# Full 128-row matmuls for the second rotary score product and for the row broadcasts of a six-layer forward pass

## The chip, the cores and the metric

The kernel runs on one core of one Trainium2 chip. The metric is the device time of one execution in microseconds; the time before is 2570.8 us, the median of three runs (2565.99 to 2572.75).

## The reference, cut to what matters

One sequence of 512 tokens, 1024 features, goes through six layers: pooling, gated delta rule, latent attention, pooling, then a layer with a state-space mixer beside a convolution, and a differential attention. All arithmetic is float32. Three of them matter here.

Latent attention (16 heads): each query and key has a part of 128 without position and a rotary part of 64; the rotary key is shared by all heads.

```python
q = jnp.concatenate([q_nope, q_rope], axis=-1)
k = jnp.concatenate([k_nope, jnp.broadcast_to(k_rope, (B, S, MLA_HEADS, MLA_ROPE))], axis=-1)
...
s = jnp.einsum('bqhd,bkhd->bhqk', q_blk, k).astype(jnp.float32) * scale
s = jnp.where(kpos[None, :] <= qpos[:, None], s, -jnp.inf)
p = jax.nn.softmax(s, axis=-1)
```

Gated delta rule (8 heads) and state-space mixer (16 heads): per head a cumulative sum over tokens of a log decay, and from it a matrix of decays between pairs of tokens.

```python
g = jnp.cumsum(g.reshape(B, N, C, H).transpose(0, 3, 1, 2), axis=-1)
diff = g[..., :, None] - g[..., None, :]
decay = jnp.exp(jnp.where(causal, diff, -jnp.inf))
```

## The kernel before, in words

Activations lie with features on the 128 partitions and the 512 tokens in the free dimension. All weights stream from HBM in slabs of 512 KB through `load_w` (L268): SyncE issues the load, ScalarE rounds the slab to a high part (L278), VectorE or GpSimd subtracts to get the low part (L279). A projection (`proj`, `projn`) calls `mm3` (L282 to L287) for every 128x128 tile of weights: high times high, high times low, low times high, each one float32r matmul. These three lines are most of TensorE's work. Plain float32 matmuls (the scores L1096, the transposes L1007, the weighted values L1011) run in two passes and show as two instructions.

The layers are written as two streams: projection units for a later head, and generators for an earlier head's attention or recurrence, which `weave` or `step` advance by a few yields after each unit. The order of instructions on each engine is then set by a planner when the program is built, from dependences and its own model of time; it also places all waits. So attention matmuls stand between the projection's matmuls on TensorE, and TensorE takes its instructions in the order that the planner wrote.

Rotary scores (`attend` in `mla`, L1084): `stacked` (L976) makes for each head of a pair one tile of 128 rows. For head i the 64 rows of its own half (`rs`) hold the high part of the rotary query, the other 64 rows its low part. `krh` and `krl` are the high and the low part of the rotary key, which stands twice in 128 rows. For each block of 128 queries three products accumulate in one bank: L1096 (128 rows, float32), L1097 (all 128 rows against `krh`: high and low query in one), and L1098 (the 64 rows `rs` against `krl`: high query times low key). With 16 heads and four query blocks each of the lines stands for 64 products, of 128, 256, 384 and 512 key columns. VectorE's mask (L1099) and the softmax wait for the third.

Row broadcasts: `cumsums` (L575) makes the cumulative sums once per layer in both layouts, and with `hi, lo` (L591 to L593) a high and a low part of the sums with one head per row and tokens in columns, 8 or 16 rows, both tiles in the buffers of the tag "rope" (three of them). `row_bcast` (L596) spreads the row of one head over 128 partitions: a stationary operand that picks the row (a column of the identity `self.sel`, repeated 128 times) times `hi` (L599), and the same times `lo` (L600) on top, into one bank of 512 columns. It is called in `k_chain` (gated delta, 8 heads, bank a), in `rec` (the same 8 heads, bank b), and in `ssd` (16 heads, bank b); `decay_t` on VectorE, or ScalarE's L1295 and L1299, read the bank.

Between `k_chain` and the recurrence lies `inverse` (L831): a chain of VectorE steps with small loads and stores through DRAM, beside which the convolutions of the projections (L552) run on VectorE too.

Of the kernel before, what the change touches and what calls it, by code (L numbers as in the profile page):

```python
# [10 lines left out]
F32 = mybir.dt.float32  # L11
F32R = mybir.dt.float32r
I32 = mybir.dt.int32
AF = mybir.ActivationFunctionType
ALU = mybir.AluOpType
# [4 lines left out]
P = 128  # L20
S = 512
# [34 lines left out]
def _consts():  # L56
    i = np.arange(P)
    ident = np.eye(P, dtype=np.float32)
    triu = (i[:, None] <= i[None, :]).astype(np.float32)
    maskt = np.where(i[:, None] <= i[None, :], 0.0, NEG).astype(np.float32)  # L60
    maskq = np.where(i[None, :] <= i[:, None], 0.0, NEG).astype(np.float32)
    lev = []
    for b in (32, 64):
        jb, ib = i[:, None] // b, i[None, :] // b
        lev.append(((jb % 2 == 0) & (ib == jb + 1)).astype(np.float32))
    b64 = ((i[:, None] // 64) == (i[None, :] // 64)).astype(np.float32)
    rc = np.zeros((P, 4, 16), np.float32)
    for n, w in enumerate(WINDOWS):
        rc[:, n, :] = 1.0 / np.minimum(np.arange(16) + 1, w)
    inv1 = (np.float32(10000.0) ** (-np.arange(32, dtype=np.float32) / np.float32(32))).astype(np.float32)  # L70
    r = i % 32
    f = (i % 64) // 32 * 16 + r % 16
    mcol = np.stack([inv1[f], np.where(r < 16, -1.0, 1.0)], 1).astype(np.float32)
    inv2 = (np.float32(500000.0) ** (np.float32(-2.0) * np.arange(8, dtype=np.float32) / np.float32(16))).astype(np.float32)
    d = i % 64
    dcol = np.stack(
        [np.where(d < 16, inv2[d % 8], 0.0), np.where(d < 8, -1.0, 1.0)], 1
    ).astype(np.float32)
    parts = [
        ("ident", ident), ("triu", triu), ("maskt", maskt), ("maskq", maskq),  # L80
        ("lev1", lev[0]), ("lev2", lev[1]), ("b64", b64),
        ("rc", rc.reshape(P, -1)),
        ("mrope", mcol), ("drope", dcol),
    ]
    return parts
# [107 lines left out]
class Net:  # L193
    def __init__(self, ctx, tc, a, poff, coff, first=()):
        self.tc, self.nc, self.a = tc, tc.nc, a
        nc = self.nc
        self.cp = ctx.enter_context(tc.tile_pool(name="cp", bufs=1))
        self.wp = ctx.enter_context(tc.tile_pool(name="wp", bufs=3))
        self.bp = ctx.enter_context(tc.tile_pool(name="bp", bufs=1))
        self.sp = ctx.enter_context(tc.tile_pool(name="sp", bufs=2))  # L200
        self.dp = ctx.enter_context(tc.tile_pool(name="dp", bufs=1, space=DRAM))
        self.pm = ctx.enter_context(tc.tile_pool(name="pm", bufs=4, space=PSUM))
        self.n = 0
        npar = a["params"].shape[1]
        ncon = a["consts"].shape[1]
        n0 = poff["norm"][1]
        par = self.cp.tile([P, npar], F32, name="par")
        con = self.cp.tile([P, ncon], F32, name="con")
        self.par, self.poff, self.con, self.coff = par, poff, con, coff
        self.x = [self.cp.tile([P, S], F32, name=f"x{i}") for i in range(8)]  # L210
        self.loaded, self.rest = [], nc.vector
        nc.sync.dma_start(par[:, :n0], a["params"][:, :n0])
        nc.sync.dma_start(self.x[0], a["xt"][0])
        ahead = [self.load_w(slab, D) for slab in first]
        self.loaded = ahead[:1]
        for i in range(1, 8):
            nc.sync.dma_start(self.x[i], a["xt"][i])
        nc.scalar.dma_start(par[:, n0:], a["params"][:, n0:])
        nc.scalar.dma_start(con, a["consts"])
        self.ones = self.cp.tile([P, P], F32, name="ones")  # L220
        nc.vector.memset(self.ones, 1.0)
        self.sel = self.cp.tile([16, 16], F32R, name="sel")
        nc.vector.tensor_copy(self.sel, self.c("ident")[:16, :16])
        self.bias = {}

    def p(self, name, i=0, n=1):
# [347 lines left out]

    def cumsums(self, gn, nh):  # L575

        nc = self.nc
        ps = self.ps("b")
        v = ps[:, : 4 * nh].rearrange("p (c h) -> p c h", c=4)
        nc.tensor.matmul(v, self.c("triu"), gn, start=True, stop=True)  # L580
        cs = self.small([P, 4, nh], "cs", 1)
        nc.vector.tensor_copy(cs, v)
        ps2 = self.ps("b")
        v2 = ps2[:, : 4 * nh].rearrange("p (c h) -> p c h", c=4)
        nc.tensor.matmul(v2, self.ones, gn, start=True, stop=True)
        last = self.small([P, 4, nh], "last", 1)
        nc.vector.tensor_copy(last, v2)
        pr = self.ps("b")
        for c in range(NC):
            nc.tensor.matmul(pr[:nh, c * P : (c + 1) * P], gn[:, c, :], self.c("triu"), start=True, stop=True)  # L590
        hi, lo = self.big("rope", F32R, [16, S]), self.big("rope", F32R, [16, S])  # L591
        nc.scalar.copy(hi[:nh], pr[:nh])
        nc.vector.tensor_tensor(lo[:nh], pr[:nh], hi[:nh].bitcast(F32), op=ALU.subtract)  # L593
        return cs, last, (hi, lo)

    def row_bcast(self, h, nh, rows, bank):  # L596
        ps = self.ps(bank)
        sel = self.sel[:nh, h : h + 1].to_broadcast([nh, P])
        self.nc.tensor.matmul(ps, sel, rows[0][:nh], start=True, stop=False)  # L599
        self.nc.tensor.matmul(ps, sel, rows[1][:nh], start=False, stop=True)  # L600
        return ps

    def decay_t(self, gb, cs, h, tag):
# [12 lines left out]
    def gdn(self, gnext):  # L616
        nc, a = self.nc, self.a
# [23 lines left out]
        cs, last, rows = self.cumsums(abn[:, :, 32:40], 8)  # L641
# [20 lines left out]
        def k_chain(heads):  # L662
            pn = self.ps("c")
            vn = pn[:, :16].rearrange("p (h c n) -> p h c n", h=4, n=1)
            for i, hd in enumerate(heads):
                kT[hd] = sil.pop(hd)
                (_, sq) = self.sq_add(None, kT[hd])
                self.tok_sums(sq, self.ones[:, 0:1], vn[:, i])
                yield 1
            ssq = self.small([P, 4, 4], "ssq", 1)  # L670
            nc.vector.tensor_scalar(ssq, vn[:, :, :, 0], EPS, None, op0=ALU.add)
            h0 = heads[0]
            nc.vector.reciprocal(bk[:, h0 : h0 + 4], ssq)
            nc.vector.tensor_tensor(
                bk[:, h0 : h0 + 4], bk[:, h0 : h0 + 4], beta.rearrange("p c h -> p h c")[:, h0 : h0 + 4], op=ALU.mult
            )
            nc.vector.tensor_copy(sk[:, h0 : h0 + 4], ssq)
            rk = self.tok_rsqrt(ssq, "rk")
            nc.vector.tensor_tensor(sk[:, h0 : h0 + 4], sk[:, h0 : h0 + 4], rk, op=ALU.mult)
            for hd in heads:  # L680
                k = kT[hd]
                gb = self.row_bcast(hd, 8, rows, "a")
                dt = self.decay_t(gb, cs, hd, "c")
                yield 1
                kk = self.ps("a")
                for c in range(NC):
                    sl = slice(c * P, c * P + P)
                    nc.tensor.matmul(kk[:, sl], k[:, sl], k[:, sl], start=True, stop=True)
                m = self.big("y")
                for c in range(NC):  # L690
                    sl = slice(c * P, c * P + P)
                    nc.vector.scalar_tensor_tensor(
                        m[:, sl], kk[:, sl], bk[:, hd, c : c + 1], dt[:, sl], op0=ALU.mult, op1=ALU.mult
                    )
                mt[hd] = m
                yield 1
# [39 lines left out]
        def rec(hd):  # L736
            st = heads.pop(hd)
            q, vN = st["q"], st["v"]
            yield 1
            gb = self.row_bcast(hd, 8, rows, "b")  # L740
            qe = self.big("c")
            nc.scalar.activation(qe, gb, AF.Exp)
            nc.vector.tensor_tensor(qe, q, qe, op=ALU.mult)
# [3 lines left out]
            for c in range(NC):  # L747
                sl = slice(c * P, c * P + P)
# [11 lines left out]
            for c in range(NC):  # L760
                sl = slice(c * P, c * P + P)
# [254 lines left out]
    def mla(self, gnext):  # L1016
        nc, a = self.nc, self.a
# [66 lines left out]
        def attend(hp, st, vN):  # L1084
            q, k = st["q"], st["k"]
            for i in range(2):
                hd = hp * 2 + i
                rs = slice(i * 64, i * 64 + 64)
                po = self.ps("c")
                vh = [v[:, (hd % 4) * P : (hd % 4) * P + P] for v in vN]  # L1090
                prev = None
                for qb in range(NC):
# [2 lines left out]
                    ps = self.ps("a")  # L1095
                    nc.tensor.matmul(ps[:, :n], q[i][:, sl], k[i][:, :n], start=True, stop=False)  # L1096
                    nc.tensor.matmul(ps[:, :n], q[2][i][:, sl], krh[:, :n], start=False, stop=False)  # L1097
                    nc.tensor.matmul(ps[:, :n], q[2][i][rs, sl], krl[rs, :n], start=False, stop=True)  # L1098
                    nc.vector.tensor_tensor(ps[:, sl], ps[:, sl], self.c("maskq"), op=ALU.add)  # L1099
                    pr, rcp = self.softmax_rows(ps, n, qs[:, qb])  # L1100
                    nc.vector.tensor_scalar(pr[:, :n], pr[:, :n], rcp, None, op0=ALU.mult)
# [40 lines left out]
    def even(self, gnext):  # L1142
# [101 lines left out]
        def ssd(g, st):  # L1244
# [42 lines left out]
            for i in range(2):  # L1287
                po = self.ps("a")
                for hh in range(2):
                    hd = 4 * g + 2 * i + hh  # L1290
                    gb = self.row_bcast(hd, 16, rows, "b")
                    w = self.big("c")
                    for c in range(NC):
                        sl = slice(c * P, c * P + P)
# [255 lines left out]
```

## Time and profile before

| | us |
|---|---|
| median of three runs | 2570.8 |
| the profiled execution | 2575.46 |
| its span, first to last instruction | 2573.7 |
| TensorE matmul busy | 2476.2 (96%) |
| TensorE weight load busy | 1976.5 (77%) |
| VectorE busy | 1628.0 (63%) |
| ScalarE busy | 1062.2 (41%) |
| GpSimd busy | 466.2 (18%) |

The mean granted clock of TensorE is 0.983 of full speed; the DMA engines move 80 GB/s on average. Busy is the union of an engine's instruction times over the span; TensorE's matmul times overlap each other, since each record holds until the modelled end of its results. By stages of the span: first pooling layer to about 320 us, gated delta to 915, latent attention to 1480 (its scores from 1100 to 1395), second pooling to 1785, state-space layer to 2245, differential attention to the end.

### The profile page before, as it was taken

How to read it: one execution, taken by the hardware profiler on the slowest of the kernel's cores; microseconds unless marked ns; L12 is line 12 of the kernel's file. 1: busy time of each engine (PE TensorE's matmuls, PEld its weight loads, DVE VectorE, ACT ScalarE, POOL GpSimd, SP SyncE). 2: the span in 40 equal slices, each digit the busy share in tenths (PEclk: the TensorE clock that was granted, in tenths of full speed). 3: DMA queues.
4: the chain of work that ended last, by engine and by line, in shares of the span. 5: the costliest groups of instructions: out<-in, count | busy, mean ns of one | idle time of the engine just before them, and what ended most of it. 6: DMA issues, size and time to landing. Idle time of an engine off the chain costs nothing. (4 is left out here: it accounts for less than half of the span.)

```text
span 2573.7 us, 30632 instructions
## 1 busy us (share of the span) xinstructions
PE 2476.2 (96%) x11692; PEld 1976.5 (77%) x11692; DVE 1628.0 (63%) x2874; ACT 1062.2 (41%) x1676; POOL 466.2 (18%) x374
## 2 busy tenths in 40 slices
PE   8999999688899999999999999999999999999999
PEld 6888877476777888887787888887777767877877
DVE  6675368678556454355557366744997888477774
ACT  4333354134335343444445332333235546365553
POOL 0121103222321110000000112203334443200000
PEclk9999999799999999999999999999999999999999
DMA  4323224311211232211111233232222211321122
GB/s 152 98 91 99 94 82 127 100 36 46 80 56 58 90 95 97 86 60 56 62 58 53 95 98 95 94 100 88 83 88 67 67 50 58 113 66 58 58 64 76
DMA packets 81907, 205.63 MB, mean 80 GB/s; under 512 B 28352, under 2 KB 28480, under 8 KB 81760
## 3 DMA queue, kind: packets, MB, share of 16 engines
q1 hardware_dynamic: 81264, 202.23, 24.7%
q8 instruction: 92, 1.51, 0.2%
q0 software_dynamic: 208, 0.66, 0.1%
q10 hardware_dynamic: 288, 0.79, 0.1%
q14 instruction: 55, 0.45, 0.1%
HBM read 196.30 MB, written 7.34 MB: 79 GB/s over the span
## 5 line engine op out<-in xcount | busy, mean ns | idle before, releaser
L285 PE MATMUL psmm<-h,wh 128*128 128x512 f32 x1704 | 691.1, 406 | 47.9 <-DVE t L552 32.0
L278 ACT CAST wh<-wr 128x1024 fp32r<-128x1024 f32 (+3 forms) x366 | 376.6, 1030 | 779.2 <-PE psmm L286 591.5
L286 PE MATMUL psmm<-h,wh 128*128 128x512 f32 x1704 | 686.5, 403 | 0.1
L287 PE MATMUL psmm<-h,wl 128*128 128x512 f32 x1704 | 684.1, 401 | 0.0
L279 DVE TENSOR_TENSOR wl<-wr,wh 128x1024 fp32r<-128x1024 f32 (+2 forms) x270 | 322.1, 1193 | 185.9 <-ACT wh L278 182.4
L285 PEld LDWEIGHTS psmm<-h,wh 128*128 128x128 f32 x1704 | 324.9, 191 | 129.6 <-issue 54.5
L287 PEld LDWEIGHTS psmm<-h,wl 128*128 128x128 f32 x1704 | 324.3, 190 | 81.8 <-issue 14.7
L285 PE MATMUL psmm<-y,wh 128*128 128x512 f32 x976 | 385.2, 395 | 0.0
L286 PE MATMUL psmm<-y,wh 128*128 128x512 f32 x976 | 384.5, 394 | 0.0
L287 PE MATMUL psmm<-y,wl 128*128 128x512 f32 x976 | 383.0, 392 | 0.0
L286 PEld LDWEIGHTS psmm<-h,wh 128*128 128x128 f32 x1704 | 324.8, 191 | 73.3 <-issue 7.7
L279 POOL TENSOR_TENSOR wl<-wr,wh 128x1024 fp32r<-128x1024 f32 (+1 forms) x96 | 237.7, 2478 | 532.6 <-ACT wh L278 410.2
L351 POOL TENSOR_TENSOR sq<-sq,sq 128x512 f32<-128x512 f32 x36 | 64.5, 1791 | 845.4 <-ACT sq L353 845.4
L285 PEld LDWEIGHTS psmm<-y,wh 128*128 128x128 f32 x976 | 183.4, 188 | 38.9 <-issue 1.6
L286 PEld LDWEIGHTS psmm<-y,wh 128*128 128x128 f32 x976 | 183.5, 188 | 37.9 <-issue 2.2
L287 PEld LDWEIGHTS psmm<-y,wl 128*128 128x128 f32 x976 | 183.4, 188 | 37.5 <-issue 0.5
L1175 DVE SCALAR_TENSOR_TENSOR psa<-y,par,psa 128x506 f32<-128x506 f32 (+28 forms) x232 | 164.9, 733 | 3.2 <-ACT psa L1171 0.9
L480 DVE TENSOR_TENSOR x<-psmm,x 128x512 f32<-128x512 f32 x44 | 30.4, 692 | 140.2 <-PE psmm L287 140.2
L996 ACT ACTIVATE c<-psa,smx,qs 128x128 f32<-128x128 f32 (+3 forms) x128 | 78.8, 616 | 88.1 <-DVE smx L994 87.5
L492 DVE TENSOR_TENSOR t<-psmm,r 128x512 f32<-128x512 f32 (+1 forms) x74 | 50.9, 688 | 100.8 <-PE psmm L287 100.7
L552 DVE SCALAR_TENSOR_TENSOR t<-psmm,par,t 128x511 f32<-128x511 f32 (+2 forms) x120 | 89.0, 743 | 7.3 <-ACT t L547 5.4
L257 ACT CAST y<-c 128x512 fp32r<-128x512 f32 x60 | 37.1, 620 | 90.3 <-POOL c L528 69.3
(362 smaller groups left out, 3343.0 us busy)
## 6 DMA issues: line engine op xcount, KB each, us to landing
wr<-in_pool_in_dram SPq DMA_DIRECT2D x64, 512.0 KB, 3.4
wr<-in_gdn_in_dram SPq DMA_DIRECT2D x48, 512.0 KB, 3.5
wr<-in_ssd_in_dram SPq DMA_DIRECT2D x48, 512.0 KB, 3.4
wr<-in_pool_out_dram SPq DMA_DIRECT2D x32, 512.0 KB, 3.4
wr<-in_mla_in_dram SPq DMA_DIRECT2D x27, 512.0 KB, 3.4
wr<-in_dif_in_dram SPq DMA_DIRECT2D x24, 512.0 KB, 3.5
wr<-in_mla_uq_dram SPq DMA_DIRECT2D x24, 384.0 KB, 3.0
wr<-in_pool_grp_dram SPq DMA_DIRECT2D x16, 512.0 KB, 3.4
```

What stands on the lines that cost most here:

```text
L257: nc.scalar.copy(hi, src)
L278: nc.scalar.copy(hi[:, :f], raw[:, :f])
L279: self.rest.tensor_tensor(lo[:, :f], raw[:, :f], hi[:, :f].bitcast(F32), op=ALU.subtract)
L285: nc.tensor.matmul(ps, wh, xh, start=start, stop=False)
L286: nc.tensor.matmul(ps, wh, xl, start=False, stop=False)
L287: nc.tensor.matmul(ps, wl, xh, start=False, stop=stop)
L351: (eng or nc.gpsimd).tensor_tensor(acc[0], acc[0], acc[1], op=ALU.add)
L480: self.nc.vector.tensor_tensor(self.x[m], ps, self.x[m], op=ALU.add)
L492: self.last = self.nc.vector.tensor_tensor(t[:n], ps[:n], r[:n], op=ALU.mult)
L552: self.last = nc.vector.scalar_tensor_tensor(t[:, s:], u[:, : S - s], w(k), t[:, s:], op0=ALU.mult, op1=ALU.add)
L996: nc.scalar.activation(pr[:, :n], ps[:, :n], AF.Exp, bias=st[:, 1:2], scale=scale, accum_out=st[:, 2:3])
L1175: nc.vector.scalar_tensor_tensor(out[:, s:], z[:, : S - s], dw(k), acc[:, s:], op0=ALU.mult, op1=ALU.add)
```

## The change

The second rotary product takes all 128 rows of the stacked query and of `krl`; it then also adds the product of the low query with the low key. The cumulative sums of a layer lie in one tile of 128 rows: the high parts from row 0, the low parts from row 32, zeros elsewhere, which a memset writes first. The selector has 128 rows and comes from the constants: column h has ones in rows h and 32 + h. One matmul over 128 rows then broadcasts a head's high and low part together.

```diff
+    sel = np.zeros((P, 16), np.float32)
+    for h in range(16):
+        sel[h, h] = sel[32 + h, h] = 1.0
...
-        self.sel = self.cp.tile([16, 16], F32R, name="sel")
-        nc.vector.tensor_copy(self.sel, self.c("ident")[:16, :16])
+        self.sel = self.cp.tile([P, 16], F32R, name="sel")
+        nc.vector.tensor_copy(self.sel, self.c("sel"))
...
-        hi, lo = self.big("rope", F32R, [16, S]), self.big("rope", F32R, [16, S])
-        nc.scalar.copy(hi[:nh], pr[:nh])
-        nc.vector.tensor_tensor(lo[:nh], pr[:nh], hi[:nh].bitcast(F32), op=ALU.subtract)
-        return cs, last, (hi, lo)
-
-    def row_bcast(self, h, nh, rows, bank):
+        rows = self.big("rope", F32R)
+        nc.vector.memset(rows.bitcast(F32), 0.0)
+        nc.scalar.copy(rows[:nh], pr[:nh])
+        nc.vector.tensor_tensor(rows[32 : 32 + nh], pr[:nh], rows[:nh].bitcast(F32), op=ALU.subtract)
+        return cs, last, rows
+
+    def row_bcast(self, h, rows, bank):
         ps = self.ps(bank)
-        sel = self.sel[:nh, h : h + 1].to_broadcast([nh, P])
-        self.nc.tensor.matmul(ps, sel, rows[0][:nh], start=True, stop=False)
-        self.nc.tensor.matmul(ps, sel, rows[1][:nh], start=False, stop=True)
+        self.nc.tensor.matmul(ps, self.sel[:, h : h + 1].to_broadcast([P, P]), rows, start=True, stop=True)
         return ps
...
-                    nc.tensor.matmul(ps[:, :n], q[2][i][rs, sl], krl[rs, :n], start=False, stop=True)
+                    nc.tensor.matmul(ps[:, :n], q[2][i][:, sl], krl[:, :n], start=False, stop=True)
```

The three calls of `row_bcast` lose the argument `nh`.

## Rows read from the trace of the kernel before

**Rows 1.** Stages: stretch, length, busy PE, PEld, DVE, ACT, POOL, clock, DMA, GB/s.
```profile
340.00:430.00 90.00, 89.22 (x435) 71.82 (x434) 64.56 (x151) 43.09 (x65) 19.02 (x15) 0.96 0.36 112
430.00:520.00 90.00, 61.98 (x272) 50.26 (x272) 61.79 (x98) 19.95 (x25) 26.68 (x14) 0.83 0.35 100
520.00:700.00 180.00, 157.43 (x811) 125.37 (x810) 129.57 (x228) 68.69 (x104) 50.67 (x31) 0.95 0.19 56
700.00:1010.00 310.00, 304.29 (x1428) 245.40 (x1427) 166.51 (x249) 129.51 (x178) 50.08 (x26) 1.00 0.24 76
...
1100.00:1395.00 295.00, 295.00 (x1570) 231.12 (x1568) 178.70 (x457) 129.89 (x277) 0.00 (x0) 1.00 0.18 57
...
1860.00:2130.00 270.00, 257.93 (x1194) 198.67 (x1193) 229.03 (x354) 127.50 (x223) 120.42 (x89) 0.96 0.20 65
```

**Rows 2.** TensorE's waits, 430 to 700 us; columns: total us, times, longest.
```profile
PE psmm L285 <- DVE t L552: 32.0, 6, 15.8
```

**Rows 3.** TensorE in order of time, 1110 to 1116 us; columns: start, duration, instruction.
```profile
1110.92 0.83 PE L1011 MATMUL psc<-h,h 128*128 128x128 f32 x6
1111.59 0.39 PE L1096 MATMUL psa<-t,t 128*128 128x128 f32 x2
...
1111.96 0.33 PE L1098 MATMUL psa<-sq,h 64*128 64x128 f32 x1
...
1112.56 0.40 PE L286 MATMUL psmm<-y,wh 128*128 128x512 f32 x1
...
1113.54 0.38 PE L1098 MATMUL psa<-sq,h 64*128 64x256 f32 x1
...
1114.19 0.40 PE L285 MATMUL psmm<-y,wh 128*128 128x512 f32 x1
...
1115.09 0.40 PE L287 MATMUL psmm<-y,wl 128*128 128x512 f32 x1
1115.32 0.40 PE L285 MATMUL psmm<-y,wh 128*128 128x512 f32 x1
```

**Rows 4.** The same view, 1119 to 1123 us.
```profile
1120.24 0.44 PE L1098 MATMUL psa<-sq,h 64*128 64x384 f32 x1
...
1120.88 1.02 PE L1096 MATMUL psa<-t,t 128*128 128x512 f32 x2
...
1122.06 0.49 PE L1098 MATMUL psa<-sq,h 64*128 64x512 f32 x1
...
1122.82 0.39 PE L286 MATMUL psmm<-y,wh 128*128 128x512 f32 x1
```

**Rows 5.** The same view, 379 to 382 us: a broadcast alone.
```profile
379.92 0.39 PE L286 MATMUL psmm<-h,wh 128*128 128x512 f32 x1
380.24 0.49 PE L599 MATMUL psa<-rope,sel 8*128 8x512 f32 x1
380.57 0.38 PE L600 MATMUL psa<-rope,sel 8*128 8x512 f32 x1
...
381.23 0.39 PE L285 MATMUL psmm<-h,wh 128*128 128x512 f32 x1
```

**Rows 6.** The same view, 2008 to 2010 us: two broadcasts together.
```profile
2008.07 0.39 PE L285 MATMUL psmm<-h,wh 128*128 128x512 f32 x1
...
2009.85 0.40 PE L287 MATMUL psmm<-h,wl 128*128 128x512 f32 x1
```

**Rows 7.** All instructions of L1098; columns: ns min/median/max, first and last start, forms.
```profile
L1098 PEld LDWEIGHTS psa<-sq,h x64: 182/183/184, 1100.9 to 1395.1; 64*128 64x128 f32 x64
L1098 PE MATMUL psa<-sq,h x64: 322/408/502, 1101.0 to 1395.1; 64*128 64x128 f32 x16, 64*128 64x256 f32 x16, 64*128 64x384 f32 x16, 64*128 64x512 f32 x16
```

**Rows 8.** The same view of L599, bank a.
```profile
L599 PE MATMUL psa<-rope,sel x8: 466/495/495, 361.9 to 423.6; 8*128 8x512 f32 x8
```

**Rows 9.** The same view of L221, the memset of the ones.
```profile
L221 DVE MEMSET ones<- x1: 165/165/165, 0.8 to 0.8; 128x128 f32 x1
```

**Rows 10.** The same view of L593, the low part of the sums.
```profile
L593 DVE TENSOR_TENSOR rope<-psb,rope x2: 678/680/681, 342.2 to 1899.0; 8x512 fp32r<-8x512 f32 x1, 16x512 fp32r<-16x512 f32 x1
```

More of the change, by code (lines that the diff above doesn't have):

```diff
@@ L81, in _consts @@
         ("lev1", lev[0]), ("lev2", lev[1]), ("b64", b64),
-        ("rc", rc.reshape(P, -1)),
+        ("rc", rc.reshape(P, -1)), ("sel", sel),
         ("mrope", mcol), ("drope", dcol),
@@ L681, in k_chain @@
                 k = kT[hd]
-                gb = self.row_bcast(hd, 8, rows, "a")
+                gb = self.row_bcast(hd, rows, "a")
                 dt = self.decay_t(gb, cs, hd, "c")
@@ L739, in rec @@
             yield 1
-            gb = self.row_bcast(hd, 8, rows, "b")
+            gb = self.row_bcast(hd, rows, "b")
             qe = self.big("c")
@@ L1087, in attend @@
                 hd = hp * 2 + i
-                rs = slice(i * 64, i * 64 + 64)
                 po = self.ps("c")
@@ L1290, in ssd @@
                     hd = 4 * g + 2 * i + hh
-                    gb = self.row_bcast(hd, 16, rows, "b")
+                    gb = self.row_bcast(hd, rows, "b")
                     w = self.big("c")
```

## The prediction

> **What bounds the kernel now.** I read the page's busy shares first, then the busy time by stage, then who waited for whom on TensorE, then the order of TensorE's instructions around the edited lines. The page gives TensorE 96% of the span (the table above); a matmul's end is modelled, so that share alone proves nothing. The stages say more [rows 1]: in the latent attention (1100 to 1395 us) TensorE is busy for all 295.00 us at the full granted clock (1.00, the 2.4 GHz level), while VectorE has work for 178.7 us and ScalarE for 129.9 us. There every microsecond that TensorE spends is on the path. The gated delta stage is mixed: full from 340 to 430 us (89.2 of 90) and from 700 on (304.3 of 310), but only 62.0 of 90 between 430 and 520 and 157.4 of 180 up to 700. TensorE waits there for VectorE's convolution line L552, 32.0 us in six waits, the longest 15.8 us [rows 2]. The state-space stage (1860 to 2130 us) has 257.9 us of 270 on TensorE with VectorE at 229.0: two engines close to their limit.
>
> What a matmul costs is read from start to start, not from its modelled duration. A 128-row matmul of 512 columns takes 0.23 us from its start to its neighbour's; a run of six 128-column ones takes 0.67 us, 0.11 each [rows 3]. Weight loads are hidden in that pace: the engine loads the next weights while the present columns stream.
>
> **Part 1: the second rotary score matmul, L1098, on 128 rows instead of 64.** The count and the columns stay; only rows change. In the trace the 64-row matmul disturbs its neighbours on both sides. From its start to the start of the second matmul behind it [rows 3, 4]:
> - 128 columns: 1111.96 to 1112.56 = 0.60 us; undisturbed it would be 0.11 + 0.23 = 0.34. Excess 0.26.
> - 256 columns: 1113.54 to 1114.19 = 0.65; undisturbed 0.12 (my value, between 0.11 and 0.23 and nearer the first) + 0.23. Excess 0.30.
> - 384 columns: 1120.24 to 1120.88 = 0.64, with two 128-column transposes behind it; undisturbed 0.17 + 0.11 + 0.11. Excess 0.25.
> - 512 columns: 1122.06 to 1122.82 = 0.76; undisturbed 0.23 + 0.23. Excess 0.30.
>
> Something is lost ahead of it as well. It can't be read there directly, since the fp32 matmul before it runs in two passes, but the broadcast shows it: L286 to L599 takes 0.32 us instead of 0.23 [rows 5], so 0.09 on entering. Per instance that is 0.35, 0.39, 0.34 and 0.39 us. The line has 16 instances of each width [rows 7]: 16 x 1.47 = 23.5 us. A check for 128 columns over the whole group, L1096 at 1111.59 to the second matmul behind: 0.97 us against 4 x 0.11 + 0.23 = 0.67, so 0.30 and not 0.35; I take 23 us. With 128 rows the neighbours have the same shape, and I see no reason for any of the excess to stay. The added arithmetic (64 more rows) costs nothing by the rows: time follows columns. All 23 us are on the path, because TensorE has no idle time in this stage [rows 1]. Next in line would be VectorE, 178.7 us in some 272: not late.
>
> A rule of the Trainium skill speaks against this part. The trace's row first: full-row matmuls with a different weight tile each follow one another at 0.23 us [rows 3], so the full-row load is not exposed. "TensorE: Matmul & The Clock Gate", section "Part 3: Packing small matmuls — row/col tiling", says that weight loads overlap running matmuls only where the row groups differ. By that rule the 64-row strips are the ones whose loads hide, and the change would expose them; this gives a rival below. The trace does not agree with it at these rows.
>
> **Part 2: row broadcasts, 32 of them, one 128-row matmul for two of 8 or 16 rows.** Alone between projections: L286 at 379.92, L599 at 380.24, second matmul behind (L285) at 381.23 [rows 5]: 1.31 us for what would be three steps of 0.23, so 0.62 saved. Two broadcasts together: 2008.07 to 2009.85 = 1.78 us [rows 6] against four steps, 0.92; 0.86 saved. There are 32 (8 into bank a [rows 8], 24 into bank b; by the code 8 heads twice and 16 heads once); the timeline has four such pairs, all in the state-space stage. So 24 x 0.62 + 4 x 0.86 = 18.3 us of TensorE time: 5.0 for the eight of the key chain (361 to 424 us), 2.5 for four heads of the recurrence before 700 us, 2.5 for four behind it, 8.4 in the state-space stage (8 x 0.62 + 3.4).
>
> Not all of it reaches the end. Behind 700 us TensorE is the bound: 2.5 counts whole. The key chain is itself TensorE-bound, but 430 to 520 us follows, where TensorE waits for VectorE [rows 1, 2]; the early half also starts that stretch's VectorE work sooner. I count half, 2.5. Up to 700 us half, 1.2. State-space: half, 4.2, because VectorE has 85% there. Together 10.4; the bounds are 2.5 (only the TensorE-bound heads) and 18.3.
>
> **Part 3: what is added.** Two memsets of 128x512 on VectorE. The trace has one of 128x128, 0.165 us [rows 9]; four times that, 0.66, is the upper bound, and nothing the lower. ScalarE's copy of the rows now waits for it, and VectorE's subtraction behind that. The rows are complete at 342.2 + 0.68 us [rows 10] while the first broadcast starts at 361.9 [rows 8], 19 us later; the wait is hidden, and I count 0. Were that cover gone: 1.3 us for both. Behind the waiting copy on ScalarE stand small exponentials that nobody needs before the recurrence. The selector's copy stays one small instruction, and the constants grow by 16 columns in one load at the start: 0. One tile of the "rope" buffers instead of two is held; nothing waits for one.
>
> **Sum.** 23 + 10.4 = 33.4, say 34 with a small gain from weight supply starting earlier that I don't price. The profiled execution took 2575.5 us (span 2573.7); 2575.5 - 34 = 2541.5. The median of the runs is 2570.8, 4.7 lower, so on its scale 2570.8 - 34 = 2537.
>
> **Rivals**, on the median's scale.
> - *Only the attention pays.* The broadcasts' 18 us vanish in the waits for VectorE, and 23 us remain: 2548. For: the waits of rows 2. Against: in two of the four stretches with broadcasts TensorE is full. Chance 0.2.
> - *Everything pays.* 23 + 18.3 = 41: 2530. For it, the key chain starts the stretch that follows. Chance 0.17.
> - *A new order eats it (slower).* The order on each engine is made at build time by a planner, and 32 matmuls fewer shift it. The place is 430 to 520 us: TensorE's projections wait for L552 because VectorE's inverse steps stand in front of it. If the new order puts one more convolution behind them, the 32.0 us of these waits double: 2570.8 - 23 - 2.5 (late heads) + 32 = 2577. It decides against the change from 34 us of added waits. For: one such wait is already 15.8 us. Against: the order would have to get worse by as much as it is bad now. Chance 0.06.
> - *Same row groups don't overlap* (the rule above). Each of the 64 loads, 0.183 us by its row [rows 7], would be exposed: +11.7; of the broadcasts the removed second matmul, 380.57 to 380.24 = 0.33 us each, -10.6 [rows 5]. 2572, no change. Chance 0.03.
> - *It doesn't do what it says*: the gaps belong to accumulating into the same bank, not to the row count, so L1098 keeps them and only broadcasts gain, 10: 2560. Against: L286 accumulates onto L285's bank at 0.23 us. Chance 0.04.
>
> **How the numbers follow.** The forecast has 0.5, 2537. The range runs from everything paid with a few us of better clock in the mixed stages (2570.8 - 46 = 2525) to two thirds of the attention's share alone (2555); spread of the runs included I give 2524 to 2556. About 0.3%, 7.7 us, is what a measurement of this kernel can tell from no change. Faster by more: forecast, both paying rivals and the bank rival, 0.91, less 0.04 for mixtures with a worse order: 0.87. Same: the rule's rival and half of those mixtures, 0.06. Slower: 0.07.
>
> **What would show it.** L1098 and the broadcast appear with 128 rows, and the second matmul behind L1098 at 512 columns starts 0.46 us after it, not 0.76: part 1 holds. The attention stage shrinks from 295 us to about 272. The broadcast becomes one step of 0.23 us. Waits for L552 stay near 32 us. Wrong: gaps around L1098 that stay, an attention stage over 285 us, or new waits of over 20 us between 430 and 700 us.

## The result, and the profile after

The changed kernel takes 2536.1 us (median of four runs, 2533.4 to 2537.9) against 2570.8 before: ratio 0.9867, 95% interval 0.985 to 0.9884. The forecast was 2537 with a range of 2524 to 2556. The total is right, and partly by luck: how it is made up is not as forecast, as the layers show.

The page's first rows for the changed kernel: 32 matmuls fewer, the busy share unchanged.

```profile
span 2536.2 us, 30574 instructions
...
PE 2439.8 (96%) x11660; PEld 1964.7 (77%) x11660; DVE 1621.5 (64%) x2876; ACT 1061.1 (42%) x1676; POOL 466.9 (18%) x374
```

Each of the first four layers ends with the same instruction, VectorE's last addition to the residual, and so does the whole. VectorE in order of time, before: ends of the first pooling, the gated delta, the attention and the second pooling layer, and of the last layer.

```profile
319.23 0.69 DVE L480 TENSOR_TENSOR x<-psmm,x 128x512 f32<-128x512 f32 x1 [3.36 <-PE psmm L287]
...
914.28 0.69 DVE L480 TENSOR_TENSOR x<-psmm,x 128x512 f32<-128x512 f32 x1 [3.35 <-PE psmm L287]
...
1476.69 0.69 DVE L480 TENSOR_TENSOR x<-psmm,x 128x512 f32<-128x512 f32 x1 [3.35 <-PE psmm L287]
...
1782.41 0.69 DVE L480 TENSOR_TENSOR x<-psmm,x 128x512 f32<-128x512 f32 x1 [6.97 <-PE psmm L287]
...
2569.77 0.69 DVE L480 TENSOR_TENSOR x<-psmm,x 128x512 f32<-128x512 f32 x1 [4.75 <-PE psmm L287]
```

The same five places after:

```profile
318.86 0.69 DVE L483 TENSOR_TENSOR x<-psmm,x 128x512 f32<-128x512 f32 x1 [3.35 <-PE psmm L290]
...
898.61 0.69 DVE L483 TENSOR_TENSOR x<-psmm,x 128x512 f32<-128x512 f32 x1 [3.36 <-PE psmm L290]
...
1445.71 0.69 DVE L483 TENSOR_TENSOR x<-psmm,x 128x512 f32<-128x512 f32 x1 [3.35 <-PE psmm L290]
...
1751.42 0.69 DVE L483 TENSOR_TENSOR x<-psmm,x 128x512 f32<-128x512 f32 x1 [6.99 <-PE psmm L290]
...
2532.26 0.69 DVE L483 TENSOR_TENSOR x<-psmm,x 128x512 f32<-128x512 f32 x1 [4.75 <-PE psmm L290]
```

By difference the gated delta layer went from 595.1 to 579.8 us, the attention layer from 562.4 to 547.1, the second pooling from 305.7 to 305.7, the last two layers from 787.4 to 780.8. That is 15.3, 15.3, 0 and 6.5 us. The prediction had 6.2, 23, nothing and 4.2: too high for the attention, too low for the gated delta layer. These differences are of two profiled executions, 37.5 us apart by their spans; the medians lie 34.7 apart.

Around the edited lines, TensorE in order of time (the rows that answer to [rows 4]):

```profile
1103.02 0.34 PE L1100 MATMUL psa<-sq,h 128*128 128x384 f32 x1
1103.20 0.38 PE L1010 MATMUL psb<-con,c 128*128 128x128 f32 x2
1103.41 1.02 PE L1098 MATMUL psa<-t,t 128*128 128x512 f32 x2
...
1104.51 0.40 PE L1100 MATMUL psa<-sq,h 128*128 128x512 f32 x1
1104.74 0.40 PE L288 MATMUL psmm<-y,wh 128*128 128x512 f32 x1
1104.97 0.40 PE L289 MATMUL psmm<-y,wh 128*128 128x512 f32 x1
```

The step that took 0.76 us at 512 columns takes 0.46 (1104.51 to 1104.97), the one of 0.64 at 384 columns 0.39. A broadcast alone, the place of [rows 5]:

```profile
378.39 0.39 PE L290 MATMUL psmm<-h,wl 128*128 128x512 f32 x1
378.61 0.40 PE L603 MATMUL psa<-rope,sel 128*128 128x512 f32 x1
378.85 0.39 PE L288 MATMUL psmm<-h,wh 128*128 128x512 f32 x1
379.08 0.40 PE L289 MATMUL psmm<-h,wh 128*128 128x512 f32 x1
```

0.69 us in place of 1.31: the 0.62 of the prediction, to the hundredth. The stages answer to [rows 1], each window at the same work:

```profile
340.00:428.00 88.00, 86.61 (x429) 72.58 (x429) 63.84 (x152) 42.91 (x65) 19.73 (x16) 0.94 0.36 114
428.00:516.00 88.00, 60.73 (x275) 49.48 (x275) 59.24 (x97) 19.48 (x25) 30.38 (x19) 0.84 0.37 102
516.00:688.00 172.00, 156.10 (x813) 124.18 (x812) 127.58 (x229) 68.89 (x105) 45.32 (x24) 0.96 0.20 59
...
1084.50:1364.00 279.50, 278.54 (x1567) 226.55 (x1566) 175.93 (x456) 129.68 (x277) 0.00 (x0) 1.00 0.19 60
```

The attention's scores take 279.5 us, not the 272 that were forecast, and TensorE now has 1 us without work there. The waits that grew are those of its weight loads (from 1080 to 1400 us), before and then after; the columns behind the colon are total us, times and longest.

```profile
PEld psc L1011 <- ACT h L1009: 3.4, 14, 0.3
...
PEld psa L1096 <- ACT c L996: 1.1, 4, 0.3
```

```profile
PEld psc L1014 <- ACT h L1012: 6.0, 21, 0.6
PEld psa L1098 <- ACT c L999: 4.7, 12, 0.6
```

The loads for the scores wait for the exponential that frees a bank, 3.6 us more than before; those for the weighted values (L1011, L1014 after) wait for ScalarE's copy of the transposed probabilities, 2.6 us more. The matmuls' own view of waits has no entry there in either kernel, so what this costs is read from their starts, further down.

### The profile page after: what moved, and what is told of

Its sections match the earlier page's. It is cut to its first block, busy times and chain, and to the rows that moved or that the text cites. A ratio compares the mean times of both kernels' runs of the same rounds, so it can differ in the third digit from the quotient of the medians.

```text
span 2536.2 us, 30574 instructions
## 1 busy us (share of the span) xinstructions
PE 2439.8 (96%) x11660; PEld 1964.7 (77%) x11660; DVE 1621.5 (64%) x2876; ACT 1061.1 (42%) x1676; POOL 466.9 (18%) x374
## 4 chain that ended last, share of the span: by engine, by line
PE 63%; DVE 4%; ACT 2%; issue 2%; POOL 1%; ACTq 0%; POOLq 0%; DVEq 0%
PE psmm L288 17%; PE psmm L290 17%; PE psmm L289 17%; PE psc L1014 2%; PE psa L1464 1%; PE psa L1098 1%; PE psb L1010 1%; DVE psa L1177 1%; ACT wh L281 1%; POOL wl L282 1%; PE psc L368 1%; PE psa L1308 0%; DVE y L261 0%; PE psb L775 0%; PE psa L1310 0%
## 5 line engine op out<-in xcount | busy, mean ns | idle before, releaser
L288 PE MATMUL psmm<-h,wh 128*128 128x512 f32 x1704 | 689.0, 404 | 46.8 <-DVE t L555 31.2
L290 PE MATMUL psmm<-h,wl 128*128 128x512 f32 x1704 | 682.7, 401 | 0.0
L290 PEld LDWEIGHTS psmm<-h,wl 128*128 128x128 f32 x1704 | 324.0, 190 | 80.0 <-issue 11.7
L290 PE MATMUL psmm<-y,wl 128*128 128x512 f32 x976 | 382.7, 392 | 0.0
L290 PEld LDWEIGHTS psmm<-y,wl 128*128 128x128 f32 x976 | 183.4, 188 | 36.9 <-issue 0.2
L555 DVE SCALAR_TENSOR_TENSOR t<-psmm,par,t 128x509 f32<-128x509 f32 (+2 forms) x120 | 89.0, 742 | 8.7 <-ACT t L550 6.2
```

Source lines behind the costliest of these rows:

```text
L288: nc.tensor.matmul(ps, wh, xh, start=start, stop=False)
L290: nc.tensor.matmul(ps, wl, xh, start=False, stop=stop)
L555: self.last = nc.vector.scalar_tensor_tensor(t[:, s:], u[:, : S - s], w(k), t[:, s:], op0=ALU.mult, op1=ALU.add)
```

## The experiments

Two facts carry these comparisons. Kernels that differ only in the rows of a matmul have the same order of instructions on every engine, as their traces show: e1 has the order of the kernel before, e2 and e3 that of the changed kernel. e4 has TensorE's order of before. And layers are compared by the residual additions shown above, one profile each. "Idle" is the time in the gated delta layer in which TensorE's matmul row is empty. "At full clock" is an estimate for that layer, its length times its mean granted clock, worked out from each trace's clock records:

| kernel | broadcast | TensorE's order | gated delta | idle | at full clock | attention | last two layers | ratio to before (95%) |
|---|---|---|---|---|---|---|---|---|
| before | 2 small | old | 595.1 | 54.9 | 567.7 | 562.4 | 787.4 | |
| e0_before_again | 2 small | old | 601.1 | 54.2 | 567.0 | 562.4 | 787.3 | 1.0006 (0.9995 to 1.0017) |
| e1 | 2 small | old | 600.7 | 55.8 | 568.3 | 547.1 | 785.7 | 0.9951 (0.9934 to 0.9968) |
| e4 | 2 of 128 rows | old | 590.6 | 56.0 | 565.0 | 548.7 | 783.3 | 0.9922 (0.9908 to 0.9935) |
| e4_again | the same | old | 591.6 | 55.4 | 564.3 | 548.7 | 783.2 | 0.9923 (0.9909 to 0.9937) |
| e3 | 1 of 64 rows | new | 580.3 | 49.5 | 559.8 | 548.7 | 785.0 | 0.9889 (0.9872 to 0.9906) |
| e3_again | the same | new | 586.3 | 49.1 | 558.9 | 548.8 | 784.7 | 0.9895 (0.9881 to 0.9909) |
| after | 1 of 128 rows | new | 579.8 | 49.0 | 554.1 | 547.1 | 780.8 | 0.9867 (0.9850 to 0.9884) |
| e0_after_again | the same | new | 582.0 | 49.0 | 554.7 | 547.1 | 781.0 | 0.9852 (0.9823 to 0.9881) |
| e2 | the same | new | 582.4 | 48.1 | 553.4 | 562.6 | 782.6 | 0.9926 (0.9908 to 0.9944) |
| e9 | 1 of 64 rows, float32 | a third | 586.1 | 47.5 | 569.0 | 548.8 | 787.5 | 0.9928 (0.9916 to 0.9941) |

The three first rows are one program in the gated delta layer, and differ by 6 us. That is TensorE's clock. From 320 to 437 us it was granted 0.97 of full speed in the first trace and 0.93 in the second (columns: stretch, length, busy PE, clock, DMA, GB/s):

```profile
320.00:437.00 117.00, 115.88 (x553) 0.97 0.33 105
320.00:437.00 117.00, 115.87 (x532) 0.93 0.31 97
```

The time at the lower level (1.2 GHz) in the layer is 54.6 us in one and 68.3 in the other. The estimate at full clock takes this out: one program then repeats within 1.3 us in every group of rows. The traces of e5, e6 and e7, which have the changed kernel's program in this layer, agree: 576.2 to 579.4 us, 49 idle, 555.0 to 555.7 at full clock. So differences of 6 us in the plain lengths of one trace are not read. The attention layer repeats within 0.1 us; the 548.7 and 548.8 of five rows against 547.1 are one spell of 3.4 us at the lower level. The same view over the whole gated delta layer, for before, e4, e3, after and e9, shows the idle times as length less busy time:

```profile
319.92:914.97 595.05, 540.11 (x2619) 0.95 0.25 76
319.62:910.24 590.62, 534.60 (x2619) 0.96 0.26 77
319.28:899.58 580.30, 530.77 (x2603) 0.96 0.26 78
319.55:899.30 579.75, 530.71 (x2603) 0.96 0.26 78
319.44:905.49 586.05, 538.53 (x2619) 0.97 0.26 77
```

**e1_rope_only and e2_bcast_only: one part each.**

```diff
e1, to before:
-  nc.tensor.matmul(ps[:, :n], q[2][i][rs, sl], krl[rs, :n], start=False, stop=True)
+  nc.tensor.matmul(ps[:, :n], q[2][i][:, sl], krl[:, :n], start=False, stop=True)
e2, to after: the same line the other way
```

> Only the second rotary score matmul on 128 rows; broadcasts as before. The instructions and their order are those of the kernel before on every engine. Theory A (changing the number of rows from one matmul to the next costs TensorE time at both sides): the attention stretch becomes 15 us shorter, as in the changed kernel, and nothing else moves; about 2555 us, 15 below before. Theory B (rows don't matter; what pays is one broadcast matmul fewer): no change, within 3 us of before. If the attention's gain depends on the rest of the change, it differs from 15 us here.

> Only the row broadcasts changed; the second rotary score matmul on 64 rows as before. The order of instructions is that of the changed kernel. If the parts add up: 37.5 - 15.3 = 22 us below before in the profiled execution (2553 us on the profile's scale), with the gated delta layer 15 us and the state-space layer 6 us shorter, and the attention stretch as long as before (295 us). If the parts share a gain, more than 22 us.

e1: the attention is 15.3 us shorter, as in the full change; the whole 12.6 us below before by the ratio. e2: the attention as before, the rest as after (the last two layers within 2 us), 19 us below. The parts add up (12.6 + 19 = 31.6 against 34.2, within the intervals).

**e3_bcast_64: one broadcast matmul on 64 rows.**

```diff
-  matmul(ps, self.sel[:, h : h + 1].to_broadcast([P, P]), rows, start=True, stop=True)
+  matmul(ps, self.sel[:64, h : h + 1].to_broadcast([64, P]), rows[:64], start=True, stop=True)
```

> The changed kernel with the one broadcast matmul on the first 64 rows instead of 128 (the zeros below are left away; the sums are the same). Order of instructions exactly that of the changed kernel. Theory A: the two row-count changes come back for 32 broadcasts, 0.09 us on entering and about 0.3 us behind, 0.4 us each, 12.5 us of TensorE time in all, of which 6 to 12 us reach the end: 2542 to 2549 us. Theory B: as fast as the changed kernel, 2536 us within 3.

2544.1 us. TensorE at the place of the broadcast above, two steps that were 0.24 and 0.23 and an entry that was 0.22:

```profile
378.96 0.39 PE L290 MATMUL psmm<-h,wl 128*128 128x512 f32 x1
379.28 0.50 PE L603 MATMUL psa<-rope,sel 64*128 64x512 f32 x1
379.70 0.50 PE L288 MATMUL psmm<-h,wh 128*128 128x512 f32 x1
380.05 0.40 PE L289 MATMUL psmm<-h,wh 128*128 128x512 f32 x1
```

1.09 us against 0.69: 0.40 for the rows alone, with the order unchanged. Theory A holds, B falls. Of 32 x 0.40 = 12.8 us between 6 and 11 reach the end (0.9889 or 0.9895 against 0.9867 or 0.9852), 4 of them in the last two layers.

> The one 64-row broadcast in the new order, a second time: its gated delta layer was as fast as that of the changed kernel in one trace (14.8 against 15.3 and 13.1 us below before), though it pays 16 times 0.4 us. If that was luck, the layer comes out 3 to 6 us longer here; if TensorE's time is hidden there, it stays at 13 to 16 us below before.

2545.4 us. The gated delta layer came out 6 us longer than in the first trace, 586.3. Its first value was luck by that much, and the luck was the clock: 41.0 us at the lower level in the first trace, 54.6 in the second. At full clock both traces have some 5 us more than the changed kernel, so that much of 16 x 0.40 = 6.4 us is paid there.

**e4_bcast_two: two broadcast matmuls of 128 rows.**

```diff
-  sel[h, h] = sel[32 + h, h] = 1.0
+  sel[h, h] = sel[32 + h, 16 + h] = 1.0        # 32 columns
...
+  for j in (0, 1):
+      sel = self.sel[:, 16 * j + h : 16 * j + h + 1].to_broadcast([P, P])
+      self.nc.tensor.matmul(ps, sel, rows, start=j == 0, stop=j == 1)
```

> The changed kernel with two 128-row matmuls for a broadcast (one selects the high row, one the low). TensorE's order is that of the kernel before, with its count of matmuls. Theory A: against the kernel before with the rotary part changed (e1) each broadcast saves only its row-count changes, 0.62 - 0.23 = 0.39 us, 12.5 us in all, most of it reaching the end; 2543 to 2549 us. Theory B: no gain from the broadcasts, about 2555 us as e1. Theory C (what the gated delta layer gained beyond the 10 us that its 16 broadcasts lose comes from the planner's new order): with the old order that layer gains no more than 16 x 0.39 = 6 us, not 15.

> Two 128-row matmuls in the old order, a second time: the gated delta layer gained 4.3 us in one trace. If the new order is worth 7 us or more there, it stays within 0 to 7 us below before.

2553.6 us both times, so theory A's 2543 to 2549 was missed: in the old order the rows alone save about 7.5 us of the whole against e1 (0.9951 to 0.9922), not most of 12.5. Theory B, no gain, falls too: beside each other e1 took 2562.5 us (2556.4 to 2563.8) and e4 2553.6 (2551.3 to 2555.5). The gated delta layer takes 590.6 and 591.6: 4 to 10 us below the three traces of the old program, and 8 to 12 above those of the new order. At full clock the rows bring 3 us, and the step from e4 to the changed kernel nearly 11. One matmul fewer, 16 x 0.23 = 3.7 us, doesn't fill that gap; TensorE's idle time does, 56 us against 49. Nor is it TensorE's work: a broadcast costs it more in e3, 1.09 us against 0.92 here (read in the same way), and yet e3's layer is 4 to 11 us shorter. Theory C holds.

**e9_bcast_64_fp32: a third order.**

```diff
+  matmul(ps, self.sel[:64, h : h + 1].bitcast(F32).to_broadcast([64, P]), rows[:64].bitcast(F32), ...)
```

> The changed kernel with the one broadcast matmul on 64 rows and in plain float32, which runs in two passes: per broadcast two row-count changes and two passes, so TensorE's cost is that of the kernel before (0.6 us above one step), while the planner, which sees one float32 matmul, writes an order of its own, neither that of before nor of after. Theory C (the order decides what the gated delta layer takes): that layer differs from both, by more than the 5.7 us between two executions of the same program. Theory A (TensorE's time decides): that layer takes what it takes before (0 to 5.7 us longer), and only the attention's 15.3 us are gained: about 2556 us.

The cost was mis-stated: a float32 pass over 512 columns takes 0.43 us, not 0.21, so a broadcast is dearer than before. The row shows the two passes; from L290 to the projection behind it is 1.37 us, where the kernel before has 0.97 (379.92 to 380.89).

```profile
371.36 0.39 PE L290 MATMUL psmm<-h,wl 128*128 128x512 f32 x1
371.68 1.12 PE L603 MATMUL psa<-rope,sel 64*128 64x512 f32 x2
372.73 0.50 PE L288 MATMUL psmm<-h,wh 128*128 128x512 f32 x1
```

With 16 x 0.4 = 6 us more work on TensorE than before, the gated delta layer takes 586.1 us, 9 to 15 below the old program. Most of that isn't the order's doing: TensorE was granted 1.00 from 340 to 428 us, and was at the lower level for 34.1 us of the layer against 54.6 to 68.3. The changed kernel's order has less in some traces as well (41.0 in e3's first), and with one trace it stays open whether this order had a part in it. At full clock the layer takes 569.0 us, as long as the old program, and the whole took 2555.0: that is theory A's forecast, 2556. What the order itself changed is the idle time, 47.5 us against 54 to 56, and those 7 us pay for the added work. So of theory C the waits are shown, not the length: this is within 4 to 6 us of the changed kernel's order. The view of TensorE's waits (330 to 850 us) shows where: the convolution's L555 (L552 before), 32.0 us in [rows 2], is down to this.

```profile
PE psmm L288 <- DVE t L555: 26.5, 6, 13.0
```

In the new order of the changed kernel it is 31.2 us, so there the shorter waits lie elsewhere: GpSimd's L921 and VectorE's L609, which held TensorE for 5.8 and 6.7 us before, take 2.2 and 4.3 in the same view. The last two layers gain nothing in e9.

**e5_probe: the cost by itself.** Behind the end of the changed kernel, rows of 24 matmuls, for instance:

```diff
+    for i in range(24):
+        mm(pa, W(i, (F, L)[i % 2]), t[(F, L)[i % 2]], start=True, stop=True)   # 128 and 64 rows in turn
```

> The changed kernel with rows of 24 float32r matmuls behind its end, one after another on an idle chip: what a change of shape costs by itself, read from start to start. Theory A (a change of the row count costs, whatever the program around it): 128 rows only, 512 columns, 0.23 us each; 128 and 64 rows in turn 0.42 us each (from 0.41 and 0.43 around L1098); 64 rows only and 16 rows only 0.23; 128 and 16 in turn 0.33 (from 0.32, 0.34, 0.31 around the broadcasts) or 0.42; 64 and 16 in turn as much as 128 and 64; 128 columns: 0.11 for one shape, 0.25 in turn. Upper and lower 64 rows in turn: 0.23 if they follow each other, less if they run side by side (the pairs of 64-row scores in the last layer look as if they did). 128 and 64 output columns in turn: about 0.31, from the step into L1306. Rival (small matmuls are slow by themselves): 64 rows only is as slow as 64 in turn with 128.

Each row of the view gives first and last start; their difference over 23 is the pace. In this order: 128 rows; 128 and 64 in turn; 64 only; lower and upper 64 in turn; 128 and 64 output columns in turn.

```profile
L1520 PE MATMUL psa<-h,h x24: 389/389/389, 2547.0 to 2552.3; 128*128 128x512 f32 x24
L1522 PE MATMUL psa<-h,h x24: 388/495/498, 2552.5 to 2562.2; 128*128 128x512 f32 x12, 64*128 64x512 f32 x12
L1524 PE MATMUL psa<-h,h x24: 383/386/394, 2562.5 to 2567.8; 64*128 64x512 f32 x24
L1526 PE MATMUL psa<-h,h x24: 385/386/499, 2567.3 to 2570.5; 64*128 64x512 f32 x24
L1538 PE MATMUL psa<-h,h x24: 388/394/398, 2624.0 to 2629.3; 128*128 128x512 f32 x12, 128*64 128x512 f32 x12
```

0.23, 0.42, 0.23, 0.14 and 0.23 us. A matmul of 64 rows is not slow; a change of rows costs 0.19 us, and an odd one among full ones has two, 0.38. The rival falls. A change of output columns costs nothing, against my 0.31; why that step was longer is open. Of the rows not shown, 128 columns took 0.11 for one shape and 0.25 in turn, as forecast, and 128 and 16 rows in turn 0.42, while the clock was at its upper level. It fell in the middle of that row, so 16 rows only (0.43) and 64 and 16 in turn (0.72) are known at the lower level alone; there 128 rows only take 0.43 as well, and 128 and 16 in turn 0.72.

**e6_no_mask: a shorter softmax chain.** The causal mask is not added to the scores.

```diff
-  nc.vector.tensor_tensor(ps[:, sl], ps[:, sl], self.c("maskq"), op=ALU.add)
```

> The changed kernel without the addition of the causal mask to the scores of the latent attention (so these scores are not masked); the chain from a score bank's last matmul to its release is one VectorE instruction of 0.3 us shorter. In the changed kernel TensorE waits 4.7 us in 12 places for the exponential that frees a score bank, against 1.1 us in 4 places before. If the attention's missing 5 us went into this chain: waits fall to 1 to 2 us and the attention stretch shortens by a further 2 to 4 us. If not: waits stay at 4 us and the stretch at 279 us.

A miss: the layer took 551.4 us, 4.3 longer, and the scores (matmuls and weight loads together) waited 9.0 us in 24 places instead of 4.7 in 12. With one VectorE instruction fewer the planner wrote another order in this layer. So the experiment doesn't price the chain.

**e7_last_layer_128: the same idea in the last layer.**

```diff
+  for i in range(2):
+      own, other = slice(i * 64, i * 64 + 64), slice(64 - i * 64, 128 - i * 64)
+      z = self.big("y")
+      nc.gpsimd.memset(z[other], 0.0)
+      nc.vector.tensor_tensor(z[own], t2[own], sh[own], op=ALU.add)
...
-  nc.tensor.matmul(ps[:, :n], q[rs, sl], k[rs, :n], start=True, stop=True)
+  nc.tensor.matmul(ps[:, :n], q[m][:, sl], k[:, :n], start=True, stop=True)
```

> The changed kernel, and the 64-row scores of the last layer on 128 rows too: the rotated query is written into two tiles, each with zeros in the other half. Theory A: the 46 groups of these scores lose 12.8 us in the changed kernel by the sum of their starts against the undisturbed pace, about 0.40 us for a pair of passes alone; that goes, VectorE's 8 more additions (0.7 us each) lie beside TensorE: 8 to 13 us below the changed kernel, about 2526 us. Rival: pairs of lower and upper rows run side by side in 18 of 64 cases and lose that, and VectorE's work delays the scores: within 5 us of the changed kernel.

2527.2 us (2522.7 to 2530.1), ratio to before 0.9814 (0.9788 to 0.9839); the changed kernel beside it took 2537.8 (2534.6 to 2540.2). Theory A holds, and the rival, within 5 us, falls. The last two layers take 770.8 us, 10 below the changed kernel, and the busy time of the last layer shows it; columns as in [rows 1], after and then e7.

```profile
2235.00:2537.00 302.00, 293.09 (x1457) 219.09 (x1455) 202.79 (x563) 154.42 (x298) 0.00 (x0) 0.99 0.20 65
```

```profile
2235.00:2526.00 291.00, 282.49 (x1455) 225.19 (x1453) 207.75 (x571) 153.77 (x298) 4.16 (x8) 1.00 0.21 68
```

VectorE's 5 us more lie beside TensorE's 10 us less.

**e0_after_again and e0_before_again: second traces.**

> The changed kernel once more, for a second trace. The attention stretch should come out 15.3 us shorter than before again; the gated delta layer, which lost 5.3 us in e1 with instructions and order equal to those of the kernel before, may differ by as much.

> The kernel before once more, for a second trace: how much the gated delta layer and the state-space layer differ between two executions of one program. From e1, whose first 1000 us are the same program: up to 6 us.

Both as expected: 15.3 us in the attention again, and 6 us between two traces of the kernel before, which begin behind the first broadcast: 4.4 us of the shift are there at 437 us, and from 612 us on it stays near 5.8.

## Why the prediction was right, point by point

- *What a row change costs.* Right, and now shown by itself: 0.19 us a change (e5), 0.40 us per broadcast at unchanged order (e3). The Trainium skill, "TensorEngine Tiling (Array Packing)", section "Tiling Modes", says that changing the tiling mode drains TensorE. It gives no figure; the trace agrees for a change of rows, with 0.19 us, though a drain can't be seen in it, and a change of output columns cost nothing. The other rule of the Trainium skill, which the prediction weighed ("TensorE: Matmul & The Clock Gate", "Part 3: Packing small matmuls — row/col tiling"), does not hold here: full-row loads of 0.19 us hide at 0.23 us a matmul (e5). The rival of 2572 us falls with it. Its step from the rule was loose as well: a 64-row strip shares row groups with the full-row matmuls around it, so by that rule its load would have been exposed before the change too.
- *Part 1, 23 us.* Mechanism right, size wrong: 15.3. The failing words are "all 23 us are on the path". Summed over all 64 places, from the matmul ahead of L1098 to the second behind it and less the undisturbed pace, 34.5 us became 13.3, so 21 were freed; my four places were a little rich. TensorE's order is the same in this layer, so its steps from start to start can be paired. Those into L1098, out of it and behind it lost 21.2 us; the others gained 5.9: 2.8 the steps to the scores' first product, 1.8 those to the weighted values, 1.4 those to the transposes of the probabilities. All three come behind the softmax or wait for a bank that it frees. The prediction looked at VectorE's busy time for the next bound, and should have looked at this chain and its banks: two for the scores. That more banks would give the 6 us back was not tested.
- *Part 2, 10.4 us.* Too low by half: by the medians 34.7 less the 12.6 to 15.3 of the attention leave 19 to 22. The 0.62 and the count were right. The gated delta layer was forecast at 3.7 + 2.5, and 15.3 came in this pair of traces, 2 of them by the clock. At full clock it is nearly 14: the rows bring 3 (the old program to e4) to 5 (e3 to after), and one matmul fewer at most 3.7. That is near the forecast, so counting half of what the early broadcasts save was not far off. The rest is a term that the sum left at nothing, the new order: TensorE's idle time there went from 54 to 56 us in all five traces of the old order to 48 to 50 in all five of the new. It is the rival of the new order with its sign turned; I had priced an order only as a loss. Which of the moved instructions does it was not isolated.
- *The state-space layer.* 4.2 forecast, 6.5 with the layer behind it. TensorE is ahead by more at first, and gives some back where it waits for a weight slab's low part from GpSimd, 2.3 us before and 4.5 after. About 3 us of the 6.5 are the clock: in these two layers 30.6 us were at the lower level in both traces of the kernel before, 23.8 in both of the changed kernel. In e1, with the small broadcasts, it is 23.8 too, so the rows are not shown to be the cause.
- *Part 3, nothing.* Right: neither memset appears in a wait.
- *Sum and chances.* The 0.6 us added for weight supply are shown by no run. By the text's own terms "same" has 0.05 and "slower" 0.08, not 0.06 and 0.07; nothing hangs on it.

So the total, 34.7 against the 34 forecast, is right by luck: 8 us too much in the attention met 9 too little in the gated delta layer, which came from its order and in part from the clock.

## What to carry to other kernels

In a stream of full matmuls one with fewer rows pays 0.19 us for going in and 0.19 for coming out, far more than the rows save; pad it with zeros if the operands can be laid out so, as e7 shows once more. Price such an edit by starts of neighbours, not by durations, then ask what each freed stretch waits for next, banks included. Where a planner orders the program, give its reordering a term of either sign (here a layer's 55 us of idle time fell by 6 to 7), and compare kernels that keep the order before believing a cause. Before reading a few us in a layer, compare the granted clock of the two traces.

## What the runs showed of the hardware that was not expected

Lower and upper halves in turn, into two banks, run side by side: 0.14 us a matmul against 0.23. In the changed kernel's last layer a lower and an upper score that stand together take as long as one alone, from the first start to the next instruction's: 0.42 against 0.41 us at 128 columns, 1.06 against 1.05 at 512. The e7 kernel gives that up and gains all the same: 36 of the 64 scores stood in such pairs, 28 alone.

TensorE's clock fell under matmuls of few rows though its matmul row shows no idle time: in e5 at 2582.7 us, while 128 and 16 rows alternated, and at 2633.9, while 128 and 64 rows alternated at 128 columns. It stayed low under 16 rows only, and rose at 2620.3 under 128 rows. The stages of e5: 128 rows at 512 columns, then 16 rows only, then 128 rows again at 512 columns, then 64 rows at 128 columns; the clock is the column behind GpSimd's.

```profile
2547.00:2552.50 5.50, 5.50 (x26) 4.52 (x25) 0.00 (x0) 0.00 (x0) 0.00 (x0) 1.00 0.00 0
...
2589.10:2599.40 10.30, 10.30 (x25) 7.47 (x23) 0.00 (x0) 0.00 (x0) 0.00 (x0) 0.50 0.00 0
...
2616.70:2623.90 7.20, 7.20 (x25) 5.79 (x25) 0.00 (x0) 0.00 (x0) 0.00 (x0) 0.75 0.00 0
...
2640.60:2645.50 4.90, 4.90 (x24) 4.90 (x25) 0.00 (x0) 0.00 (x0) 0.00 (x0) 0.50 0.00 0
```

At 0.50 (the 1.2 GHz level) 16 rows of 512 columns take 0.43 us each, as 128 rows do there. Whether broadcasts of 8 and 16 rows helped to lower the clock inside the kernel is open: the whole run's granted clock was 0.983 before and 0.985 after.
